# A swap of 16-partition blocks by small SBUF to SBUF transfers instead of a VectorE shuffle

## The chip, the core and the metric

One core of a Trainium2 chip runs the whole program. Its engines are TensorE (PE in the profile, with its weight loads as PEld), VectorE (DVE), ScalarE (ACT), GpSimd (POOL) and SyncE (SP); in this kernel all transfers are issued on SP's queue. The metric is the device time of one execution in microseconds (us). A profiled execution gives a trace beside its time.

## The reference

Two layers of an encoder trunk on 1024 tokens of width 1024, float32. Each layer: a norm and one combined projection; then three groups side by side (attention with 8 query and 2 key heads, a two-way gated recurrence, a convolution module); an output projection with a residual; and a feed-forward part of width 4096 with a residual. The rotary part acts on queries and keys ahead of attention:

```python
def _rotate(x, cos, sin):
    half = x.shape[-1] // 2
    x1, x2 = x[..., :half], x[..., half:]
    c, s = cos[None, :, None, :], sin[None, :, None, :]
    return jnp.concatenate([x1 * c - x2 * s, x1 * s + x2 * c], axis=-1)

def apply_axial_rope(x, row_cs, col_cs):
    xf = x.astype(jnp.float32)
    out = jnp.concatenate([_rotate(xf[..., :ROPE_AXIS_DIM], *row_cs),
                           _rotate(xf[..., ROPE_AXIS_DIM:], *col_cs)], axis=-1)
    return out.astype(x.dtype)
```

A head has 64 numbers: 32 are rotated by the token's row, 32 by its column. In each 32 the first 16 are paired with the last 16. So the rotation needs, beside x, a copy of x in which the two blocks of 16 have changed places.

## The kernel before

Activations lie transposed: channels on the 128 partitions, the 1024 tokens along the free axis. A tile of 128 channels is two heads, so a block of 16 channels is a block of 16 partitions, and the swap that the rotation needs goes across partitions.

A layer starts with the combined projection, made in 20 columns of 128 channels in the order `ZORDER`. For each, `wtile` loads the weights (L196, into one of two "raw" buffers), splits them into a high and a low part (L199 on ACT, L200 on DVE or POOL), and `dense_steps` (L223) makes three passes of matmuls into one of two PSUM tiles "S".

Around the rotary part four pieces of work are interleaved by generators, one step at a time. `h0.core()` is the recurrence of the first two heads: score matmuls L502 into PSUM banks "e" and "c", masked copies L513, decays L533 and L534 (on POOL and DVE), scaled copies L490, transposes L547 copied out by L548. `qkv()` makes the columns for values, keys and four query tiles and calls `vpart`, `kpart` and `qpart`. `conv_all()` is the convolution, whose 31 taps per tile (L357 and L349) run on DVE. The loop takes two steps of `qkv` and two of the convolution for each step of `h0.core()`:

```python
qg = qkv()
for _ in h0.core():
    for g in (qg, cg, qg, cg):
        next(g, None)
```

`rope` is called five times a layer: once by `kpart`, four times by `qpart`, on a whole tile of 128 x 1024. `kpart` takes the tile from PSUM (L327), squares it (L659), sums the squares per head on TensorE (`tok_sums`, L162), computes the reciprocal root in `rstd` (L151 to L156, small DVE instructions), spreads it over a tile on ACT (`widen`, L168), scales the key on POOL (L664), calls `rope`, multiplies by the spread statistics that TensorE has transposed into a bank "e" (`flip`, L178, then L668), and stores the tile in DRAM (L669). `qpart` takes the squares (L678) and the scaled query (L679) from PSUM, computes the sums and the reciprocal root (used later as `nqc`, L686 to L688), calls `rope`, and stores the tile (L693). Attention loads keys (L721, L722) and queries (L737) from DRAM later.

`rope` itself is four instructions: the shuffle into `sh` (L629, DVE), x times cosine in place (L630, POOL), `sh` times sine (L631, DVE), and their sum (L632, DVE). `sh` is one of four buffers of the tag "tmp", which `kpart`, `qpart`, `widen` and most other parts share; "e" and "c" have two banks each.

No order of engines is written out by hand here. The tile framework draws up, when the program is built, the order of the instructions on each engine and queue, the assignment of the buffers and the waits; on the chip each engine runs its list in that order. The attention stage and the feed-forward part follow, the latter with some orders fixed by added dependencies.

## Time and profile before

| | |
|---|---|
| Time, median of 3 runs | 2532.92 us (2527.47 to 2532.97) |
| The profiled execution | 2533.45 us, of it 2531.7 us span |
| Mean granted TensorE clock | 0.990 |
| Busy: PE, DVE, ACT, POOL | 2455.4, 2003.8, 1204.2, 723.3 us |
| Instructions | 34044 |
| Packets of the transfers, bytes | 113077, 286.99 MB |

The span runs from the first to the last instruction. A row of a timeline gives the start in us, the duration, the engine, the line of the kernel, the operation, what it writes and reads, and in square brackets how long the engine was idle before and what ended that. A row of waits gives who waited for whom, the sum in us, how many times, and the longest. Rows of SPq are issues on SP's queue; "to landing" is the time from an issue to the arrival of its data.

### The profile page before, as it was taken

What the parts mean: (1) busy time and instruction counts of PE and PEld (TensorE: products, weight loads), DVE (VectorE), ACT (ScalarE), POOL (GpSimd) and SP (SyncE); (2) the same over time, 40 slices, a digit from 0 to 9 for tenths busy, and PEclk for the clock granted to TensorE, in tenths of its full rate; (3) what the DMA queues carried; (4) which work ended last, traced back from release to release, by engine and by line L of the source; (5) the groups of instructions that cost most, each with busy time, mean ns of one, the idle gap of its engine ahead of it and who ended that gap; (6) DMA issues with size and microseconds to landing.
All of it is one profiled execution on the core that took longest, in us unless ns stands there. A gap on an engine that the chain in (4) does not pass through costs nothing. (4 is left out here: it accounts for less than half of the span.)

```text
span 2531.7 us, 34044 instructions
## 1 busy us (share of the span) xinstructions
PE 2455.4 (97%) x12608; PEld 2017.4 (80%) x12608; DVE 2003.8 (79%) x3051; ACT 1204.2 (48%) x1960; POOL 723.3 (29%) x463
## 2 busy tenths in 40 slices
PE   8999899999999999999999998999999999999999
PEld 7777778878788887888887777788787888878887
DVE  6999689862887778987859995998638877789886
ACT  4222478763544444443523215787635444444332
POOL 0232556533034330000123225564330344200000
PEclk9999999999999999999999999999999999999999
DMA  4102300032254458554221113000322444574442
GB/s 163 55 34 71 104 17 18 26 119 90 91 179 142 150 175 298 163 175 158 76 100 42 45 60 104 18 20 24 133 92 89 169 140 163 186 280 158 162 151 91
DMA packets 113077, 286.99 MB, mean 113 GB/s; under 512 B 11408, under 2 KB 11664, under 8 KB 112912
## 3 DMA queue, kind: packets, MB, share of 16 engines
q1 hardware_dynamic: 112912, 284.83, 32.5%
q8 instruction: 99, 1.62, 0.3%
q14 instruction: 66, 0.54, 0.1%
HBM read 197.75 MB, written 87.03 MB: 112 GB/s over the span
## 5 line engine op out<-in xcount | busy, mean ns | idle before, releaser
L223 PE MATMUL S<-xs,whi 128*128 128x512 f32 x1280 | 361.1, 402 | 8.7 <-ACT whi L199 7.4
L223 PEld LDWEIGHTS S<-xs,whi 128*128 128x128 f32 x1280 | 241.0, 191 | 63.8 <-ACT whi L199 7.4
L1204 PE MATMUL S<-xs,xs 128*128 128x512 f32 x816 | 201.6, 390 | 2.6 <-DVE xs L905 2.6
L223 PE MATMUL S<-xs,wlo 128*128 128x512 f32 x640 | 201.9, 396 | 0.0
L904 ACT ACTIVATE xs<-m 128x512 fp32r<-128x512 f32 x216 | 126.0, 619 | 141.7 <-DVE m L915 48.8
L769 POOL TENSOR_SCALAR P<-P,mx 128x1024 f32<-128x1024 f32 x124 | 141.3, 1140 | 163.0 <-DVE mx L768 116.0
L795 DVE TENSOR_TENSOR PT<-c,PT 128x512 fp32r<-128x512 f32 x256 | 170.5, 683 | 21.1 <-ACT PT L794 19.6
L1204 PEld LDWEIGHTS S<-xs,xs 128*128 128x128 f32 x816 | 152.8, 188 | 35.4 <-DVE xs L905 3.4
L794 ACT ACTIVATE PT<-c 128x512 fp32r<-128x512 f32 x256 | 148.4, 592 | 68.3 <-PE c L790 65.1
L357 DVE SCALAR_TENSOR_TENSOR x<-x,par,x 128x1009 f32<-128x1009 f32 (+14 forms) x120 | 172.3, 1436 | 1.6
L811 PE MATMUL e<-PT,x 128*128 128x256 f32 x1024 | 170.8, 297 | 1.4 <-ACT PT L794 1.1
L199 ACT ACTIVATE whi<-raw 128x1024 fp32r<-128x1024 f32 x56 | 59.1, 1057 | 233.0 <-PE S L223 214.0
L764 DVE TENSOR_SCALAR_CACHE_REDUCE P<-S,nqc 128x1024 f32<-128x1024 f32 x124 | 158.6, 1279 | 14.1 <-PE S L753 10.1
L790 PE MATMUL c<-cons,P 128*128 128x128 f32 x992 | 152.0, 277 | 12.0 <-POOL P L769 7.1
L905 DVE TENSOR_TENSOR xs<-m,xs 128x512 fp32r<-128x512 f32 x216 | 144.7, 693 | 22.1 <-ACT xs L904 22.0
L753 PE MATMUL S<-x,QS 128*128 128x512 f32 x480 | 152.1, 419 | 8.1 <-DVE P L764 7.9
L767 ACT ACTIVATE P<-P,mx 128x1024 f32<-128x1024 f32 x124 | 142.4, 1148 | 28.0 <-DVE P L764 25.8
L261 POOL TENSOR_TENSOR tmp<-tmp,tmp 128x1024 f32<-128x1024 f32 x19 | 50.7, 2666 | 361.4 <-ACT tmp L260 361.2
L811 PEld LDWEIGHTS e<-PT,x 128*128 128x128 f32 x1024 | 137.2, 191 | 11.1 <-ACT PT L794 3.4
L790 PEld LDWEIGHTS c<-cons,P 128*128 128x128 f32 x992 | 113.2, 140 | 40.8 <-POOL P L769 11.9
L223 PEld LDWEIGHTS S<-xs,wlo 128*128 128x128 f32 x640 | 122.1, 191 | 26.7 <-issue 0.4
L1204 PE MATMUL e<-xs,xs 128*128 128x512 f32 x552 | 141.0, 390 | 1.3 <-ACT xs L904 0.9
(310 smaller groups left out, 5632.7 us busy)
## 6 DMA issues: line engine op xcount, KB each, us to landing
m<-ad SPq DMA_DIRECT2D x104, 512.0 KB, 3.8
ad<-x SPq DMA_DIRECT2D x176, 256.0 KB, 2.2
raw<-w_in_t SPq DMA_DIRECT2D x40, 512.0 KB, 3.4
xs<-w_t SPq DMA_DIRECT2D x36, 512.0 KB, 3.7
raw<-w_t SPq DMA_DIRECT2D x36, 512.0 KB, 3.6
m<-w_t SPq DMA_DIRECT2D x32, 512.0 KB, 6.7
ad<-tmp SPq DMA_DIRECT2D x48, 256.0 KB, 2.1
x<-w_t SPq DMA_DIRECT2D x24, 512.0 KB, 4.8
```

Of the source, the lines that this page charges most:

```text
L223: nc.tensor.matmul(zp[h] if type(zp) is list else zp[:, h, :], w, xx[:, h * 512 : (h + 1) * 512], start=first, stop=last)
L357: nc.vector.scalar_tensor_tensor(y[:, lo:hi], u[:, lo + d : hi + d], par[:, l, wof + tap : wof + tap + 1], y[:, lo:hi], op0=ALU.mult, op1= ...
L753: nc.tensor.matmul(S[:, hb, :], qs, kk[:, hb * 512 : (hb + 1) * 512], start=first, stop=not first)
L764: nc.vector.tensor_scalar(Pt, S, nqc[:, j, ci : ci + 1], 3.0e38, op0=ALU.mult, op1=ALU.min, accum_out=mx[:, 1:2])
L767: nc.scalar.activation(Pt, Pt, AF.Exp, bias=mx[:, 1:2], scale=-1.0, accum_out=mx[:, 2:3])
L769: nc.gpsimd.tensor_scalar(Pt, Pt, mx[:, 3:4], 0.0, op0=ALU.mult, op1=ALU.add)
L790: nc.tensor.transpose(t[:, q * P : (q + 1) * P], Pt[:, hb, q * P : (q + 1) * P], ident)
L794: nc.scalar.activation(hi, src, AF.Copy)
L795: nc.vector.tensor_tensor(lo, src, hi.bitcast(F32), op=ALU.subtract)
L811: nc.tensor.matmul(pvp[:, cs], VS[g][:, hb * 4 + kb, :], pt[:, kb, :], start=hb == 0 and n == 0, stop=hb == 1 and n == 7,)
L905: ordered("v", nc.vector.tensor_tensor(lo, src, hi.bitcast(F32), op=ALU.subtract))
L1204: nc.tensor.matmul(banks[dt], w[i][:, dt * P : (dt + 1) * P], a[j], start=n == 0 and name not in ("M6", "M7", "M3"), stop=n == 3 * SG - 1, ...
```

## The change

The shuffle within each group of 32 partitions goes. In its place SP issues eight transfers from SBUF to SBUF; each copies 16 partitions by 1024 float32 numbers, 64 KB, and the block from partition b goes to partition b with bit 16 turned over. The multiply L630 overwrites x in place, so it comes after all eight copies have read x; L631 comes after all eight have written `sh`.

```diff
         nc.sync.dma_start(ropeS, rope_d[1])
-        swap = [(i + 16) % 32 for i in range(32)]
-
         def rope(x):
             sh = tmp()
-            nc.vector.stream_shuffle(sh, x, swap)
+            for b in range(0, P, 16):
+                nc.sync.dma_start(sh[b : b + 16], x[b ^ 16 : (b ^ 16) + 16])
             nc.gpsimd.tensor_tensor(x, x, ropeC, op=ALU.mult)
             nc.vector.tensor_tensor(sh, sh, ropeS, op=ALU.mult)
             nc.vector.tensor_tensor(x, x, sh, op=ALU.add)
```

## The prediction

> **What bounds the kernel now.** I read the page's first lines and its chain first, then the stretches around the changed lines, then who waits for whom there.

> ```profile
> span 2531.7 us, 34044 instructions
> ...
> PE 2455.4 (97%) x12608; PEld 2017.4 (80%) x12608; DVE 2003.8 (79%) x3051; ACT 1204.2 (48%) x1960; POOL 723.3 (29%) x463
> ...
> PE 37%; DVE 4%; ACT 1%; issue 1%; POOL 1%; DMA 0%; SPq 0%; POOLq 0%; DVEq 0%; ACTq 0%
> ```

> TensorE carries the kernel: 97% busy, and nearly all of the chain that was followed back is PE. The chain names no DMA. So what matters is whether the change lets PE run dry, or fills a gap that PE has. The rotary part runs at about 165 to 250 us (first layer) and 1412 to 1507 us (second). The busy time of these stretches (columns: PE, PEld, DVE, ACT, POOL, granted clock, DMA share, GB/s):

> ```profile
> 165.00:265.00 100.00, 92.00 (x638) 74.52 (x638) 93.03 (x164) 24.96 (x31) 27.67 (x11) 0.98 0.20 69
> ...
> 1437.00:1470.00 33.00, 30.35 (x200) 25.70 (x200) 29.15 (x58) 10.69 (x16) 11.86 (x6) 0.84 0.19 72
> 1470.00:1505.00 35.00, 35.00 (x282) 27.62 (x280) 30.44 (x58) 5.53 (x7) 7.54 (x2) 0.95 0.13 46
> ```

> PE and DVE are both about 90% busy here, so either can end a wait. PE's own waits in this stage, in the first layer (165 to 270 us) and then the second (1400 to 1530 us):

> ```profile
> PE e L178 <- ACT tmp L168: 2.8, 1, 2.8
> PE c L547 <- ACT T L548: 2.7, 1, 2.7
> PE e L502 <- DVE tmp L668: 2.0, 1, 2.0
> ```

> ```profile
> PE e L502 <- DVE tmp L668: 2.0, 1, 2.0
> PE c L547 <- ACT T L548: 1.4, 1, 1.4
> PE e L178 <- ACT tmp L168: 1.2, 1, 1.2
> ```

> They add to 7.5 and 4.6 us, 12.1 together. That is the most that a faster rotary part could give back. One of them is the rotary part itself: L502 needs a PSUM bank "e" that L668, the end of the key's rotary part, still reads.

> **What is removed.** Ten shuffles:

> ```profile
> L629 DVE STREAM_SHUFFLE tmp<-tmp x10: 1281/1318/1349, 170.6 to 1499.4; 128x1024 f32<-128x1024 f32 x10
> ```

> ```profile
> L357 DVE SCALAR_TENSOR_TENSOR x<-x,par,x 128x1009 f32<-128x1009 f32 (+14 forms) x120 | 172.3, 1436 | 1.6
> ```

> 10 x 1.318 = 13.2 us of DVE work, 6.6 per layer. DVE fills its time here with the convolution's taps (L357), which are needed much later, so most of it only brings taps forward. Outright gain on the path: I take 0, bounds 0 and the 12.1 above.

> **What is added.** Eighty copies of 16 partitions, 64 KB each, on SP's queue. The trace has no SBUF to SBUF copy; the nearest rows are the partial loads that SP issues, 128 KB (L737) and 256 KB in half the partitions (L721):

> ```profile
> L737 SPq DMA_DIRECT2D tmp<-qd x60: 444/562/599, 300.8 to 1762.6; - x60
> ...
> DMA to landing us min/median/max: 2.5/2.8/4.2
> ```

> ```profile
> L721 SPq DMA_DIRECT2D tmp<-kd x4: 450/450/451, 259.8 to 1559.9; - x4
> ...
> DMA to landing us min/median/max: 4.0/4.4/4.7
> ```

> From the first issue to the last landing a tile takes seven issue intervals and one landing: 7 x 0.562 + 2.8 = 6.7 us. The bounds are 7 x 0.444 + 2.5 = 5.6 and 7 x 0.599 + 4.7 = 8.9. I take 6.7, since 128 KB is nearest in size. Against the shuffle's 1.32 that is 5.4 us more latency per tile, and 4.5 us of SP per tile.

> SP's queue is passed by the weight loads (L196). The tightest is this one, and its user:

> ```profile
> 1455.67 0.34 SPq L196 DMA_DIRECT2D raw<-w_in_t  x1
> ```

> ```profile
> 1464.96 1.06 ACT L199 ACTIVATE whi<-raw 128x1024 fp32r<-128x1024 f32 x1 [7.55 <-PE S L223]
> ```

> 9.3 us lie between. Eight copies ahead of it (4.5 us) and a landing of 2.8 leave 2 us, so the load stays hidden; uncovered it would cost PE up to 4.5 less those 2. I take 0. POOL's multiply L630 overwrites x and so must wait until all copies have read it; POOL is 12 of 33 us busy there, so what is queued behind it waits little.

> **The key tile (one per layer).** This is where latency meets PE. Rows of POOL, ACT and DVE in the second layer, and the chain's own pieces:

> ```profile
> 1410.90 1.92 POOL L664 TENSOR_SCALAR tmp<-tmp,par 128x1024 f32<-128x1024 f32 x1 [13.72 <-ACT tmp L659]
> ...
> 1429.28 3.29 POOL L630 TENSOR_TENSOR tmp<-tmp,x 128x1024 f32<-128x1024 f32 x1 [13.38 <-issue]
> ```

> ```profile
> 1426.76 1.06 ACT L168 ACTIVATE tmp<-nwy 128x1024 f32<-128x1024 f32 x1 [3.46 <-DVE nwy L156]
> ```

> ```profile
> 1427.84 1.31 DVE L629 STREAM_SHUFFLE tmp<-tmp 128x1024 f32<-128x1024 f32 x1
> ...
> 1430.22 3.43 DVE L631 TENSOR_TENSOR tmp<-tmp,x 128x1024 f32<-128x1024 f32 x1
> ...
> 1434.76 1.21 DVE L632 TENSOR_TENSOR tmp<-tmp,tmp 128x1024 f32<-128x1024 f32 x1
> ...
> 1437.09 1.27 DVE L668 TENSOR_TENSOR tmp<-tmp,e 128x512 f32<-128x512 f32 x2
> ```

> ```profile
> 1437.82 2.67 PE e L502 x15
> 1440.49 3.71 PE S L223 x8
> ```

> The key was ready at 1412.8, yet its shuffle ran at 1427.84, right after L168 had taken its buffer from the same four "tmp" buffers that the shuffle's output comes from; the code takes L168's first. I read this as: the buffer, not DVE, held the shuffle, and it will hold the copies as well. Then the copies leave at about 1427.8 and land at 1434.5. After that come L630's 3.3 us, with L631 beside it ending about 1.1 later (as at 1432.6 and 1433.7), L632's 1.2, and L668: 1427.8 + 6.7 + 3.3 + 1.1 + 1.2 = 1440.1 against 1437.1. With the convolution taps between them kept, up to 5.4 us later. PE already waits 2.0 here, but the eight dense matmuls that now run behind L502 (3.7 us) and the next column's can be put ahead. I take +1.0 per layer, since that cover is larger than the 3.0; uncovered it is 3.0 to 5.4. Below nothing: -2.0, if the copies leave early.

> [...]

> **The query tiles.** Their results are stored and read much later, so only DVE's and POOL's own order counts.

> ```profile
> 1448.68 1.11 ACT L679 ACTIVATE tmp<-S,par 128x1024 f32<-128x1024 f32 x1 [5.05 <-PE e L162]
> ...
> 1485.52 1.10 ACT L679 ACTIVATE tmp<-S,par 128x1024 f32<-128x1024 f32 x1
> ```

> ```profile
> 1448.71 1.22 DVE L632 TENSOR_TENSOR tmp<-tmp,tmp 128x1024 f32<-128x1024 f32 x1
> ...
> 1456.58 1.34 DVE L629 STREAM_SHUFFLE tmp<-tmp 128x1024 f32<-128x1024 f32 x1
> ...
> 1457.98 1.21 DVE L631 TENSOR_TENSOR tmp<-tmp,x 128x1024 f32<-128x1024 f32 x1
> ...
> 1499.40 1.34 DVE L629 STREAM_SHUFFLE tmp<-tmp 128x1024 f32<-128x1024 f32 x1
> ...
> 1501.96 1.22 DVE L631 TENSOR_TENSOR tmp<-tmp,x 128x1024 f32<-128x1024 f32 x1
> ...
> 1505.52 1.23 DVE L632 TENSOR_TENSOR tmp<-tmp,tmp 128x1024 f32<-128x1024 f32 x1
> ```

> Tile 1 is ready at 1449.8, when L632 of tile 0 frees a buffer (1449.9, some 3 later after the key's delay). Landing: 1453 + 6.7 = 1459.7, against L631 at 1458.0: DVE stands 1.7 us and saves 1.34, so +0.4 per layer, bounds -1.3 and +5.4. Tile 3: the copies replace the shuffle at 1499.4 and land at 1506.1, so L631's 1.2 us moves from a time when DVE has room into the stretch 1505 to 1519 that ends in PE's wait for L168; half of it, +0.6, bounds -1.3 and +3.4 (1.2 and the collision's 2.2). Tiles 0 and 2 stand before DVE work that fills with taps: 0, bounds -1.3 and +5.4.

> **Sum.** Per layer 1.0 + 0.4 + 0.6 = 2.0; two layers +4.0. The profiled execution took 2533.45 us (its span and 1.75 around it), 0.5 over the median 2532.92 of the three runs. 2533.45 + 4.0 = 2537.45, less that 0.5: **2537 us**. A change within 0.3% (7.6 us) can't be told from none here, so this is "same".

> **The rivals.**
> - *Copies leave early.* If they start when the key is ready (1412.8), they land at 1419.5 and L668 comes before PE needs its bank: 2 x 2.0 saved, and part of the other 8.1 us of waits as DVE is 13.2 us lighter. Between 2529 and 2521, say 2525. For it: nothing in SP's queue stands there. Against: the shuffle itself could have run at 1412.8 and did not. Chance 0.14.
> - *All hidden.* The dense columns cover everything: 2533. For it: PE was 35.00 of 35.00 us busy from 1470. Chance 0.27.
> - *DVE stands at the landing (slower).* DVE runs in a fixed order; if that order was drawn up for a shorter copy than the chip gives, DVE stops at L631 with score masks and decays behind it, which PE waits for. Price 5.4 us per tile; it decides when the landing comes over 1.5 us after DVE gets there. On the key, tile 1 and tile 3 of both layers, 6 x 5.4 = 32 at most, half of it on PE's path or more: 2549 to 2565, say 2557. For it: L547 and L178 already wait on DVE chains. Against: taps to fill with. Chance 0.20.
> - *The copies go one after another.* Each pays its own landing: 8 x 2.8 = 22 us a tile, 21 more than the shuffle; on six tiles 126, half covered: about 2600. Against it: L721 and L722 fill two halves of one tile, issued 0.5 us apart, with landings of 4.4 and 4.9 us. Chance 0.04. [...]

> **How the numbers follow.** The forecast itself (2534 to 2541) has 0.35. Faster by over 0.3%, below 2525.3: most of the first rival, 0.12. Slower, above 2540.5: the third and fourth and the forecast's upper tail, 0.33. Same: 0.55. The range takes in the first rival's middle and most of the third's: 2525 to 2557.

> **What would show it.** In the changed profile: DVE's 13.2 us gone; the copies of a tile issued about 0.56 apart and landed 6.7 after the first; L631 and L630 released by DMA; the key's copies issued only after L168; PE's wait for L668 between 2 and 5 us. The prediction is wrong if the copies leave when the key is ready, if PE's order changes so that other waits than these appear, or if DVE's idle time before L631 sums to over 15 us.

## The result, and the profile after

2563.64 us (median of four, 2562.62 to 2566.46) against 2531.36 before: a ratio of 1.0132, 95% interval 1.0114 to 1.0149. The change makes the kernel slower by some 32 us. The prediction was 2537 (2525 to 2557, most likely "same"): the change cost more than it allowed for.

The page of the changed kernel, its first lines; the profiled execution took 2563.92 us:

```profile
span 2562.1 us, 34240 instructions
...
PE 2474.2 (97%) x12608; PEld 2036.4 (79%) x12608; DVE 1991.6 (78%) x3031; ACT 1204.5 (47%) x1960; POOL 710.7 (28%) x463
```

The span grew by 30.4 us. PE executes the same 12608 matmuls, but is busy with them for 18.8 us longer (2455.4 to 2474.2); the other 11.6 us are idle PE (76.3 to 87.9). So the larger share is not waiting: the same matmuls take longer. Line numbers from L630 of before on are one smaller now: cosine L629, sine L630, sum L631, key's last multiply L667; the copies are L628.

All copies, and in the first layer the key tile's on SP behind a weight load, POOL's cosine multiply (its 18.15 us of idle time ended by their landing), and DVE:

```profile
L628 SPq DMA_DIRECT2D tmp<-tmp x80: 507/587/1492, 169.8 to 1534.2; - x80
...
DMA to landing us min/median/max: 2.2/2.3/4.4
```

```profile
169.40 0.33 SPq L196 DMA_DIRECT2D raw<-w_in_t  x1
169.82 5.03 SPq L628 DMA_DIRECT2D tmp<-tmp  x8
```

```profile
176.78 2.69 POOL L629 TENSOR_TENSOR tmp<-tmp,x 128x1024 f32<-128x1024 f32 x1 [18.15 <-DMA tmp<-tmp]
```

```profile
169.37 12.50 DVE L357 SCALAR_TENSOR_TENSOR x<-x,par,x 128x1016 f32<-128x1016 f32 x8
181.79 1.22 DVE L200 TENSOR_TENSOR wlo<-raw,whi 128x1024 fp32r<-128x1024 f32 x1
182.93 5.23 DVE L357 SCALAR_TENSOR_TENSOR x<-x,par,x 128x1023 f32<-128x1023 f32 x4
188.07 1.22 DVE L630 TENSOR_TENSOR tmp<-tmp,x 128x1024 f32<-128x1024 f32 x1
189.21 1.27 DVE L357 SCALAR_TENSOR_TENSOR x<-x,par,x 128x1019 f32<-128x1019 f32 x1
190.40 1.22 DVE L631 TENSOR_TENSOR tmp<-tmp,tmp 128x1024 f32<-128x1024 f32 x1
191.54 1.27 DVE L357 SCALAR_TENSOR_TENSOR x<-x,par,x 128x1018 f32<-128x1018 f32 x1
192.72 1.28 DVE L667 TENSOR_TENSOR tmp<-tmp,e 128x512 f32<-128x512 f32 x2
```

The copies are done 7.0 us after the first issue (169.82 to 176.78). Yet DVE reaches the sine multiply only at 188.07, 18.25 us after the first issue, of which it is busy for 17.89: twelve convolution taps and a weight split stand ahead of it in DVE's list. The key's end (L667) moves from 179.86 in the kernel before to 192.72. The bank it holds keeps PE, in each layer:

```profile
PE e L502 <- DVE tmp L667: 7.9, 2, 3.9
```

What follows is seen in the granted clock (the column after POOL), first 180 to 220 us before, then 190 to 220 us after:

```profile
180.00:190.00 10.00, 9.02 (x64) 7.70 (x66) 8.25 (x11) 3.10 (x5) 6.38 (x3) 0.83 0.14 54
190.00:200.00 10.00, 10.00 (x89) 8.68 (x91) 10.00 (x25) 4.05 (x6) 2.89 (x3) 1.00 0.39 131
200.00:210.00 10.00, 7.54 (x44) 5.95 (x40) 10.00 (x21) 2.35 (x3) 2.61 (x1) 1.00 0.14 54
210.00:220.00 10.00, 9.73 (x86) 8.32 (x88) 9.88 (x14) 2.68 (x5) 3.35 (x1) 1.00 0.16 52
```

```profile
190.00:200.00 10.00, 6.04 (x40) 5.62 (x40) 8.73 (x12) 3.14 (x7) 2.03 (x2) 0.58 0.44 105
200.00:210.00 10.00, 10.00 (x65) 8.83 (x65) 6.58 (x13) 3.53 (x5) 4.33 (x4) 0.56 0.01 2
210.00:220.00 10.00, 10.00 (x48) 8.44 (x48) 7.72 (x24) 0.13 (x1) 0.35 (x1) 0.66 0.13 22
```

A row gives a mean; in windows of half a microsecond the clock is 1.00 or 0.50, apart from those in which it changes. The kernel before has a fall here too: behind its gap of 2.0 us the clock is 0.50 from 181.8 to 185.2. After the change it is 0.50 from 191.7 to 208.7, and again from 212.1 to 219.0, though PE is busy without a pause from 200 to 220. The recurrence's score matmuls right behind the gap, same line and shape (minimum/median/maximum in ns), before and after:

```profile
L502 PE MATMUL e<-m,m x64: 272/272/419, 180.6 to 200.2; 64*128 64x128 f32 x64
```

```profile
L502 PE MATMUL e<-m,m x32: 417/418/577, 193.5 to 198.9; 64*128 64x128 f32 x32
```

The query tiles carry the delay on. Their stores leave SP at 219.86, 237.83, 256.07 and 275.25 instead of 191.29, 205.19, 222.81 and 247.98, and attention's first score matmuls then wait for PSUM tiles that DVE empties late:

```profile
PE S L752 <- DVE tmp L327: 10.6, 2, 5.4
PE S L752 <- DVE m L327: 8.0, 2, 4.3
```

The second layer's key statistics are spread (L168) at 1444.71 instead of 1426.76, so the first layer has cost 18 us; the other 12 fall in the second.

### The profile page after: what moved, and what is told of

It is laid out like the page before. It is cut to its first block, busy times and chain, and to the rows that moved or that the text cites. A ratio compares the mean times of both kernels' runs of the same rounds, so it can differ in the third digit from the quotient of the medians.

```text
span 2562.1 us, 34240 instructions
## 1 busy us (share of the span) xinstructions
PE 2474.2 (97%) x12608; PEld 2036.4 (79%) x12608; DVE 1991.6 (78%) x3031; ACT 1204.5 (47%) x1960; POOL 710.7 (28%) x463
## 5 line engine op out<-in xcount | busy, mean ns | idle before, releaser
L223 PE MATMUL S<-xs,whi 128*128 128x512 f32 x1280 | 362.8, 404 | 11.8 <-ACT whi L199 7.7
L223 PEld LDWEIGHTS S<-xs,whi 128*128 128x128 f32 x1280 | 244.7, 193 | 68.3 <-ACT whi L199 7.7
L223 PE MATMUL S<-xs,wlo 128*128 128x512 f32 x640 | 202.3, 397 | 0.0
L794 DVE TENSOR_TENSOR PT<-c,PT 128x512 fp32r<-128x512 f32 x256 | 170.7, 683 | 22.9 <-ACT PT L793 21.4
L357 DVE SCALAR_TENSOR_TENSOR x<-x,par,x 128x1009 f32<-128x1009 f32 (+14 forms) x120 | 173.0, 1442 | 2.3
L763 DVE TENSOR_SCALAR_CACHE_REDUCE P<-S,nqc 128x1024 f32<-128x1024 f32 x124 | 158.6, 1279 | 14.5 <-PE S L752 10.1
L199 ACT ACTIVATE whi<-raw 128x1024 fp32r<-128x1024 f32 x56 | 59.1, 1058 | 235.0 <-PE S L223 215.9
L810 PEld LDWEIGHTS e<-PT,x 128*128 128x128 f32 x1024 | 136.5, 190 | 12.1 <-ACT PT L793 4.6
L789 PEld LDWEIGHTS c<-cons,P 128*128 128x128 f32 x992 | 113.1, 140 | 40.7 <-POOL P L768 11.6
L223 PEld LDWEIGHTS S<-xs,wlo 128*128 128x128 f32 x640 | 122.1, 191 | 25.6
```

The lines of the kernel that those rows point to most:

```text
L223: nc.tensor.matmul(zp[h] if type(zp) is list else zp[:, h, :], w, xx[:, h * 512 : (h + 1) * 512], start=first, stop=last)
L357: nc.vector.scalar_tensor_tensor(y[:, lo:hi], u[:, lo + d : hi + d], par[:, l, wof + tap : wof + tap + 1], y[:, lo:hi], op0=ALU.mult, op1= ...
L763: nc.vector.tensor_scalar(Pt, S, nqc[:, j, ci : ci + 1], 3.0e38, op0=ALU.mult, op1=ALU.min, accum_out=mx[:, 1:2])
L789: nc.tensor.transpose(t[:, q * P : (q + 1) * P], Pt[:, hb, q * P : (q + 1) * P], ident)
L794: nc.vector.tensor_tensor(lo, src, hi.bitcast(F32), op=ALU.subtract)
L810: nc.tensor.matmul(pvp[:, cs], VS[g][:, hb * 4 + kb, :], pt[:, kb, :], start=hb == 0 and n == 0, stop=hb == 1 and n == 7,)
```

## The experiments

The theories in the texts on record: **A**, the key's late end holds a bank, PE runs dry and its clock falls; **B**, the query tiles pass the delay on through SP's queue and the four "tmp" buffers; **C**, the sine multiply's place in DVE's list, drawn up when the program is built, lies far behind the landing; **D**, the chip's own issue and landing times make it late. Each ratio is against runs of the kernel before on the same chip, with its 95% interval. "PE busy" and "PE idle" are those of the profiled execution, less before's 2455.4 and 76.3; the time beside them is the median of several executions. Every edit has the framework draw up all lists anew, so no run moves one instruction alone.

**key_only** and **query_only**: which tiles cost it.

```diff
-            nc.vector.stream_shuffle(sh, x, swap)
+            if key:                      # query_only: if not key
+                for b in range(0, P, 16):
+                    nc.sync.dma_start(sh[b : b + 16], x[b ^ 16 : (b ^ 16) + 16])
+            else:
+                nc.vector.stream_shuffle(sh, x, swap)
```

> Only the key tile's swap (one per layer) is made by the eight copies; the four query tiles keep the shuffle. Theory A (the key's end L667 comes some 13 us later, holds its PSUM bank, TensorE stands 4 us twice, and its granted clock falls for 25 to 30 us after): most of the 32 us is here, 2550 to 2563 us, with PE's wait for L667 near 4 us and the granted clock below 0.7 behind it. Theory B (the query tiles hand their delay on to one another through SP's queue and the four tmp buffers, so that the keys' loads and attention start late): 2531 to 2540 us.

> Only the four query tiles' swaps are made by copies; the key keeps the shuffle. Theory A: at most a third of the 32 us, 2531 to 2542 us. Theory B: 2550 to 2563 us, with the last query store some 20 us later than before.

key_only: 2550.33 us, 1.0055 (1.0035 to 1.0075); PE busy +9.5, idle +2.2 in the profiled execution, the shortest of its four (2545.15). The key's first issue is at 170.98, its sine multiply at 189.25, PE's wait 3.91, and the clock 0.70 and 0.62 from 190 to 210. query_only: 2544.76 us, 1.0038 (1.0024 to 1.0052), between the ranges of both theories; PE busy +4.3, idle +8.3, with the key's wait as before (2.0) and this one at attention's start:

```profile
PE S L757 <- DVE m L327: 6.9, 1, 6.9
```

Both parts cost, and together (16 + 10 us) somewhat less than the whole change; the rest would then come from having both, which no run shows. A and B both stand, neither alone; by which path the query tiles pass their delay on, no run separates.

**one_transfer**, **four_copies**, **two_queues**, **act_queue**, **three_queues**: does the chip make the sine multiply late, or its place in the list? The same 512 KB in one and in four transfers; then the eight copies on SP and ACT in turn, all on ACT, or on SP, ACT and POOL in turn.

```diff
-            for b in range(0, P, 16):
-                nc.sync.dma_start(sh[b : b + 16], x[b ^ 16 : (b ^ 16) + 16])
# one_transfer
+            nc.sync.dma_start(sh, x)
# four_copies
+            for b in range(0, P, 32):
+                nc.sync.dma_start(sh[b : b + 32], x[b : b + 32])
# two_queues: (nc.scalar if b % 32 else nc.sync); act_queue: nc.scalar
# three_queues: (nc.sync, nc.scalar, nc.gpsimd)[b // 16 % 3]
```

> One transfer of all 128 partitions (512 KB) from x to sh stands in place of the eight copies; it does not swap the blocks, so the rotation's values are not computed. If it is the number of copies that costs (their 5 us of issue, and the place in the engines' order that follows from eight of them): 2528 to 2542 us, L630 within 6 us of the issue. If any transfer in this place costs the same (its round trip, its waits and the buffers it holds): 2550 us or more.

> Four copies of 32 partitions each, block to the same block, so the swap is not made and the rotation's values are not computed; otherwise the changed kernel. Theory C (the order drawn up for the engines counts about 2.3 us for each copy, one after another, and puts the multiply L630 that far behind the first copy, whatever the chip needs): L630 on the key tile about 9 to 11 us after the first issue, against 18 with eight and 5 with one, and the time between: 2538 to 2552 us. Rival D (the chip's own issue and landing make the delay): L630 2 to 3 us earlier than with eight copies, 2555 us or more.

> The eight copies as in the changed kernel, four issued by SyncE and four by ScalarE, in turn. Theory C: the order counts four on each queue, L630 9 to 12 us after the first issue, 2538 to 2554 us. Rival D: the landing comes some 2 us earlier, 2555 to 2563 us. Rival E (each of the eight waits counts, not the queue): L630 at 18 us as before and no gain, 2560 us or more.

> All eight copies of each tile are issued by ScalarE, none by SyncE. Theory C: eight on one queue as before, L630 16 to 20 us behind the first issue, 2552 to 2568 us. Rival S (the copies hold up weight loads, stores and key loads on SP's queue): 2533 to 2546 us.

> The eight copies of a tile go to three queues in turn: three on SyncE, three on ScalarE, two on GpSimd; nothing else differs from the changed kernel. Theory C (the sine multiply stands where the drawn-up order expects the copies to be done, so its distance from the first issue goes with the longest row of copies on one queue): one queue gave 18.25 us for eight in a row, two queues 12.3 us for four in a row, one transfer 4.8 us; the straight line through them, about 2 to 3 us for each further copy in a row, gives 9 to 10 us here, the key's last multiply at 183 to 185 us, and a time between the single transfer's and the two queues', 2537 to 2546 us. A rival, theory S (what counts is an engine's own queue standing behind the issues): eight on ScalarE gave a wait of 10 us on TensorE, and GpSimd, which also does the cosine multiply of the same tile, now issues two copies ahead of it; by it the time is at or above that of two queues, 2548 us or more, with the distance short all the same.

| | Time, ratio (95%) | First issue to POOL's start | First issue to sine multiply | PE busy, idle |
|---|---|---|---|---|
| one_transfer | 2535.99, 1.0006 (0.9992 to 1.0019) | 4.8 | 4.8 | +11.1, -3.6 |
| four_copies | 2544.27, 1.0050 (1.0036 to 1.0063) | 5.8 | 12.0 | +8.7, +1.6 |
| two_queues | 2548.26, 1.0056 (1.0038 to 1.0074) | 6.5 | 12.3 | +16.7, -2.9 |
| the change | 2563.64, 1.0132 (1.0114 to 1.0149) | 7.0 | 18.25 | +18.8, +11.6 |
| act_queue | 2590.52, 1.0215 (1.0199 to 1.0231) | 7.1 | 17.6 | +23.3, +33.4 |
| three_queues | 2565.83, 1.0114 (1.0090 to 1.0139) | 5.5 | 11.0 | +30.5, +2.0 |

In one_transfer the profiled execution is the longest of its ten (2541.03). In three_queues the distances are counted from ACT's first issue. four_copies, SP, POOL and DVE:

```profile
L628 SPq DMA_DIRECT2D tmp<-tmp x4: 578/604/857, 170.1 to 172.0; - x4
```

```profile
175.92 2.50 POOL L629 TENSOR_TENSOR tmp<-tmp,x 128x1024 f32<-128x1024 f32 x1 [17.02 <-DMA tmp<-tmp]
```

```profile
182.04 1.22 DVE L630 TENSOR_TENSOR tmp<-tmp,x 128x1024 f32<-128x1024 f32 x1
```

The landing moves by 2.2 us between one transfer and eight, the sine multiply by 13. This refutes D and supports C: DVE's place for it goes with the number of transfers behind each other on a queue, and in all but the single transfer the data lie there 5 to 11 us before. The distances of four_copies and two_queues are a little above what C gave (9 to 11 and 9 to 12), their times inside it.

act_queue, whose time missed both ranges, shows another cost: the eight issues stand in ACT's own queue, and ACT does no other work for the 17.5 us up to 197.60, when the next tile's copies have been issued. The key ends as in the change (192.35), but PE's dense work ends at 182.8, and its wait for the key grows to 10.3 us.

three_queues missed theory C's time, which was 2537 to 2546. The sine multiply is early (11.0 us behind ACT's first issue, little above the 9 to 10 expected; POOL's two copies were issued before, at 159.9) and the key ends at 186.4. Its time is at least that of two queues, as the rival said, but the rival's reason isn't seen: PE's wait for the key is 1.9 us. PE is idle 2.0 us more than before, and the time is lost in busy PE:

```profile
190.00:225.00 35.00, 35.00 (x146) 28.83 (x146) 20.47 (x45) 8.45 (x13) 10.08 (x8) 0.50 0.16 47
```

35 us without a gap at half the clock. The dense product's matmuls (L223) in 188 to 222 us, before and in three_queues:

```profile
L223 PE MATMUL S<-xs,whi x51: 387/393/498, 191.6 to 221.7; 128*128 128x512 f32 x51
```

```profile
L223 PE MATMUL S<-xs,whi x15: 628/628/793, 190.4 to 221.7; 128*128 128x512 f32 x15
```

So the clock is a price of its own beside the waits. The fall follows a gap of 1.9 us (185.3 to 187.2), with dense matmuls ahead of it and thin ones (L502) behind. The gap alone doesn't explain it: the kernel before has one of 2.0 us at the same place, and its clock is back after 3.4 us. Nor does an early sine multiply alone give the time back.

**scaled_first**, **before_scaled_first**: is the held bank the whole of A? The key is multiplied by its statistics ahead of its rotary part, so the bank is free early; once from the changed kernel, once from the kernel before.

```diff
-            rope(kz)
             for h in range(2):
                 sl = kz[:, h * 512 : (h + 1) * 512]
                 nc.vector.tensor_tensor(sl, sl, flip(krw, h), op=ALU.mult)
+            rope(kz)
```

> All ten swaps by copies as in the changed kernel, but the key is multiplied by its statistics (the multiply that reads the PSUM bank) ahead of the rotation and not behind it, so that the bank is free before the copies begin. The result is the same, since the factor is one number per head and token. Theory A: PE's wait for the bank and the fall of the clock behind it go, 2531 to 2547 us. Theory B: 2553 to 2565 us.

> The kernel before, with its shuffle, and the key multiplied by its statistics ahead of the rotation. PE's wait of 2.0 us for the bank in each layer goes: 2525 to 2532 us if nothing takes its place, 2533 or more if the tmp buffers then end that wait.

scaled_first: 2560.5 us, 1.0094 (1.0070 to 1.0118), inside theory B's range. The multiply that frees the bank runs at 172.09, but a gap of 3.53 us comes back one step later, where the query's sums L162 wait for ACT's L677, which waits for a "tmp" buffer. The clock still falls (0.79, 0.53). before_scaled_first: 2537.71, 1.0018 (1.0007 to 1.0029); PE's wait of 2.0 us goes, and one of 1.3 us for a masked copy (L513) comes. So the bank is one way in which the delay reaches PE; with it gone in the changed kernel, the four buffers are the next.

**forced_order**: the list changed by hand. The convolution tap that the program makes next after a rotary part is placed behind the rotary part's last DVE instruction (for the key, its last multiply).

```diff
-                nc.vector.scalar_tensor_tensor(
+                tapped = nc.vector.scalar_tensor_tensor(
...
+                if pend:
+                    tc.add_manual_dep(tapped.ins, pend.pop().ins.name, mybir.DependencyInfo(
+                        mybir.DependencyClass.NoSync, mybir.DependencyReason.DATA), reason="order")
...
-            nc.vector.tensor_tensor(x, x, sh, op=ALU.add)
+            pend[:] = [nc.vector.tensor_tensor(x, x, sh, op=ALU.add)]
```

> The changed kernel with one more order: the convolution tap that the code makes next after a rotation may not stand ahead of the rotation's last DVE instruction (for the key, the multiply that reads the bank). The copies are as they were. Theory C: on the chip the key's L630 follows the landing, about 8 us after the first issue and not 18, PE's wait for the bank is below 3 us, and 2540 to 2555 us; the query tiles, which stand behind score work and not behind taps, gain little. Rival D: L630 does not come earlier, 2560 us or more.

2614.09 us, 1.0316 (1.0298 to 1.0334): a clear miss. The key's part did come early (sine multiply 174.63, 10.1 us behind the first issue; last multiply 177.21, no wait of PE for it), but other work went late. PE's waits in the first layer:

```profile
PE e L595 <- DVE m L570: 12.7, 2, 11.4
PE e L162 <- POOL tmp L377: 8.5, 1, 8.5
PE c L551 <- DVE A L517: 3.6, 1, 3.6
```

An order fixed at one place is paid at others. It isn't settled what a better complete order could give.

**copies_beside**, **small_copies**: do the copies cost something by themselves? In both the shuffle stays. The first adds eight copies of 256 bytes that nobody reads; the second lets eight copies of eight columns write into `sh` behind the shuffle.

```diff
             nc.vector.stream_shuffle(sh, x, swap)
# copies_beside
+            nc.vector.tensor_copy(scr[:, 0:1], sh[:, 0:1])
+            for b in range(0, P, 16):
+                nc.sync.dma_start(scr[b : b + 16], ropeS[b ^ 16 : (b ^ 16) + 16, 0:4])
# small_copies
+            for b in range(0, P, 16):
+                nc.sync.dma_start(sh[b : b + 16, 0:8], x[b ^ 16 : (b ^ 16) + 16, 0:8])
```

> The kernel before with its shuffle, and after each shuffle eight small copies on SP's queue, from the sine table to a spare column block that nobody reads (16 bytes of each partition), released by a copy of one column of the shuffle's output. SP's 4 to 5 us of issue per tile are there, and nothing waits for them. Theory C (the place that the order gives to the instructions behind the copies): within 0.3% of before, 2528 to 2540 us. Rival S (SP's queue, with weight and key loads behind the copies): 2542 us or more.

> The kernel before with its shuffle, and then eight copies that write the first 8 columns of the shuffle's output once more with the same values: the copies' number, queue and waits are those of the changed kernel, their bytes 1/128. Theory C: the bytes do not matter, L630's counterpart stands 16 to 20 us behind the first copy's issue on the key tile, 2553 to 2568 us. Rival B2 (the bytes): 2530 to 2540 us.

copies_beside: 2546.12 us, 1.0042 (1.0022 to 1.0061), above theory C's range and inside rival S's (2542 or more), so S isn't refuted. Its ten executions spread from 2537.71 to 2556.92 at clocks of 0.990 to 0.982. The profiled one (2538.78) is among the shortest and shows much the same waits as the kernel before, so no trace shows what the other 7 us pay for. small_copies: 2577.01, 1.0168 (1.0151 to 1.0185), more than the change. The distance is only 6.3 us here (first issue 172.07, sine multiply 178.39): it goes with the bytes as well as with the number, and a fixed 2.3 us for each copy in the framework's order is refuted. Its loss, with the key's sine multiply early, is outside both ranges and again mostly clock: PE busy +29.1, idle +10.8; 0.78, 0.50 and 0.53 from 190 to 220, behind gaps of 2.1 us (up to 185.97) and 1.7 us (up to 193.40). The longest wait comes later, up to 279.96:

```profile
PE e L178 <- ACT tmp L168: 10.5, 5, 5.3
```

**late_key**, **late_all**: is lateness enough, with no transfer at all? The shuffle stays; GpSimd multiplies its result by one, eight times on the key tile (late_key), and five times on each query tile besides (late_all).

```diff
             nc.vector.stream_shuffle(sh, x, swap)
+            for _ in range(late):       # key 8; queries 0 (late_key), 5 (late_all)
+                nc.gpsimd.tensor_scalar(sh, sh, 1.0, 0.0, op0=ALU.mult, op1=ALU.add)
```

> The kernel before, with its shuffles, and on the key tile alone eight further GpSimd instructions on the shuffled tile (multiply by one, add nothing), which put off the sine multiply as the copies did; no transfer is added, and the values are unchanged. Eight by 1.92 us is 15.4 us, so the sine multiply comes some 17 us behind the shuffle's start (18.25 in the changed kernel), with GpSimd at most half busy there. Theory A (a late key is enough: it holds its bank, TensorE thins out, the granted clock falls): the key's last multiply at 189 to 194 us, granted clock below 0.8 for some 20 us after it, 2540 to 2552 us, as the run with copies on the key alone (2550). Rival T (the transfers themselves cost it: their packets, and SyncE's queue standing in issues): without them 2528 to 2537 us and a clock as before, late key or not.

> As the last, with the eight further GpSimd instructions on the key tile and five on each of the four query tiles (9.6 us each; GpSimd then has 28 + 54 of some 105 us in this stretch). No transfer is added. Theory A with B (all tiles late, and with them the four buffers): 2550 to 2570 us, as the changed kernel, TensorE's busy time 10 to 25 us above that of before at the same number of matmuls. Rival T: under 2540 us.

late_key: 2555.08 us, 1.0087 (1.0056 to 1.0119), some 3 us above theory A's range; key_only had 1.0055 (1.0035 to 1.0075). late_all: 2588.03, 1.0213 (1.0184 to 1.0243), PE busy +22.9, idle +28.6, also above A's range. late_key's sine multiply and last multiply, PE's wait, and the clock:

```profile
189.34 1.23 DVE L633 TENSOR_TENSOR tmp<-tmp,x 128x1024 f32<-128x1024 f32 x1 [3.19 <-POOL tmp L631]
...
194.01 1.27 DVE L670 TENSOR_TENSOR tmp<-tmp,e 128x512 f32<-128x512 f32 x2
```

```profile
PE e L502 <- DVE tmp L670: 8.7, 1, 8.7
```

```profile
190.00:200.00 10.00, 5.17 (x22) 4.49 (x23) 10.00 (x12) 2.30 (x5) 3.35 (x2) 0.57 0.14 54
200.00:210.00 10.00, 9.65 (x83) 7.98 (x83) 8.37 (x16) 3.72 (x4) 3.42 (x2) 0.92 0.13 52
```

Without a transfer added, a key as late costs about as much time as with the copies: lateness is enough, and the rival, that the transfers themselves are needed for it, is refuted. But the loss is made up otherwise. The profiled execution, the shortest of five (2547.10), has 12.3 us more of idle PE and 1.3 of busy PE, where key_only's has 2.2 and 9.5; PE's wait is 8.7 us and not 3.9, and the clock is low for 10 us in a row, not the 20 expected. That the slow clock comes from a late key is therefore not shown by this run. late_all's waits are longer than the change's, so the change isn't rebuilt in size by it. The five executions of late_key, one and the same list of instructions, took 2547.10 to 2563.57 us at mean clocks of 0.988 to 0.982: longer goes with lower.

## Why the prediction was wrong

- *The copies' price.* Right. 0.587 us an issue and 7.0 us from first issue to POOL's start, against 0.562 and 6.7. No wait of PE for split weights grew by more than 0.3 us. DVE lost 12.2 us of busy time for 13.2 of shuffles.
- *The buffer gate.* Its time came out, its reason not: the key's copies left at 169.82, not when the key was ready, but 0.42 us behind a weight load (L196) that stood ahead of them on SP's queue and had waited 9.8 us for its own buffer. In three_queues POOL issued two of the key's copies at 159.9, 10.9 us before L168 ran, so in that list at least the "tmp" buffer was free by then. No run takes SP's order away.
- *The key tile, the step that failed.* The sum 1427.8 + 6.7 + 3.3 + 1.1 + 1.2 kept DVE's list of before: it has DVE take the sine multiply as soon as POOL starts, and asked only how late the landing is. It should have asked where the list puts the instruction: 18.25 us behind the first issue, 11.3 behind the landing. The key's end moved by 12.9 us (179.86 to 192.72), not by 3.0 to 5.4. PE's wait (3.9) is still inside the 2 to 5 given, but only since PE's order moved too: that part came out by luck.
- *The cover.* "Eight dense matmuls" were to hide the delay at +1.0 per layer. PE did have more dense work ahead (120 matmuls of L223 from 160 to 190, 79 before), and then nearly none: 4 from 193 to 216, against 55 before. Cover spent early is missing later.
- *The clock, a missing term.* All prices were idle time at the clock of before, although the prediction's own row for 1437 to 1470 us, behind the same wait for L668, has a granted clock of 0.84. 18.8 of the 30.4 us are slower matmuls. In the first layer, 180 to 225 us, PE was busy for 41.29 us with 321 matmuls at 0.96, then for 40.67 us with 224 at 0.73.
- *The query tiles.* +0.4 and +0.6 were too small: the stores leave 27 to 33 us late, and attention waits 5.4 and 4.3 us for PSUM tiles where before it waited 0.4 and 1.5. Alone they cost 10 us (query_only). With that one of the prediction's own signs of being wrong came: PE's order changed, and other waits than the listed ones appeared.
- *The rivals.* "DVE stands at the landing" came nearest in time (2549 to 2565) for a reason that turned out opposite: the list has the sine multiply well behind the chip's landing, not ahead of it, and DVE never stood there; that its time was near is luck. "One after another" did not happen: eight copies landed within 7.0 us, where eight landings in a row would be 8 x 2.3 = 18.4. One transfer of the same bytes was quicker than the eight, 4.8 us. The 2.2 us that the bound of +3.4 for tile 3 counts for a collision of sine and cosine multiply are shown by no run as a price of the change: its ten sine multiplies took 1.216 to 1.230 us, each begun 4.4 to 8.6 us after POOL's multiply had ended. In the kernel before, one begun 1.0 us into POOL's multiply took 3.42 (173.01) and one begun 0.1 us ahead of it 1.22 (199.13); no run varies that alone.

What stays open: the exact cost that the framework's order gives a copy, what decides how long the clock stays low, what copies_beside pays for, and why three_queues and small_copies lose as much or more with an early key. The late key is shown to be enough for about half of the loss, not to be needed for a loss of this size.

## What to carry to other kernels

Where a program's order is drawn up ahead, price an operation by where its user will stand in the engine's list, not by when its data land: a DVE that never stands can still be 11 us late. Here eight small transfers in place of one VectorE instruction saved 1.3 us of that engine and put the use of the result 15 us later (173.01 to 188.07); without slack behind it, that was a loss, and a single transfer (which does no swap) only reached parity. And compare PE's busy time at the same number of matmuls: if it grows, as here by 18.8 us, look at the granted clock: no list of waits shows that loss.

## What the runs showed of the hardware

How long it stayed low didn't go with the gap ahead: 2.0 us before and in query_only, 1.9 us in three_queues, 3.9 us in the change, 8.7 us in late_key. Where eight product matmuls (L223) stood in a row right behind the first sixteen of L502 (before, late_key, act_queue), it was back 5 to 7 us after PE resumed. Where more thin ones (L502, L162) came first or between (key_only, query_only, the change, three_queues), it was back after 13 to 38 us. This is read off the traces; no run varies it alone.

A fall came 2.0 us into the change's gap of 3.9 us, behind gaps of 1.9 us (three_queues) and 2.0 us (before), and at 212.1 in the change with PE busy by the records. In three_queues PE was busy by the records for the 35 us from 190 to 225, all of them at 0.50. What sets off a fall and what ends it isn't shown.
